# Input stage of a hybrid attention block: x tiles 6 and 7 load into a free buffer, ahead of the turned blocks

## The chip, the cores and the metric

The kernel runs on one NeuronCore of a Trainium2 chip. The metric is the time of the whole launch in microseconds (us) on the device, the median of several runs. Five engines run their own instruction streams in order: TensorE (PE in the profile, PEld for its weight loads), VectorE (DVE), ScalarE (ACT), GpSimd (POOL) and SyncE (SP), which here issues nearly all DMAs. They meet by semaphores.

## The reference

One layer over x of 2048 rows by 1024 columns:

```python
h = rms_norm(x, norm_gain[layer])
proj = h @ w_in[layer]
qa, ka, va, qb, kb, vb, ga, gb, mg = jnp.split(proj, split_idx, axis=-1)
...
ya = ya.reshape(bsz, S, A_WIDTH) * jax.nn.silu(ga)
...
merged = gates[:, :, 0] * br_a + gates[:, :, 1] * br_b
x = x + merged @ w_out[layer]
```

Between the split and the gates lie two attention mixers with normed q and k. What matters here comes before them: each row of x is scaled by one over its root mean square, each column by a gain, and the result h, transposed, is the operand of every projection; and the first of these projections is that of the gate path `silu(ga)`.

## The kernel before, in words

The program has an input stage, then 14 units of attention (projection, norm, scores, output), then the merge and output projection. All tensors that TensorE multiplies are split in two fp16 parts, high and low, and each product is three matmuls (high by high, high by low, low by high). The input stage makes the transposed, normed h in two tensors, XH (high) and XL (low), in four quarters of 512 rows of x, and runs 16 gate products with them: quarter q by gate weight c is gate 4q + c, 24 matmuls each (8 of XH by the weight's high part gh, 8 of XH by its low part gl, 8 of XL by gh). SP loads x twice: as 16 tiles `xt` of 128 rows (x 0 to 15, 512 KB each), and already transposed as "turned blocks" `xq` (t1, t2, t3: one for each of the quarters 1 to 3, four loads of 512 KB each). Names of the steps, with their lines in the profile:

- **sq.t**: ScalarE squares x tile t and sums along its rows (L492; tile 3 on VectorE, L488). **st, ln, nw**: mean, and one over the root, for a quarter's four tiles (L496, L264 and L265, L278 to L280; in quarters 2 and 3 all on VectorE, L509 to L513).
- **dg.t**: that scale on the diagonal of a 128 by 128 tile (L523 on ScalarE, L521 for the first quarter).
- Quarter 0 has no turned block: TensorE turns x tiles 0 to 3 by a matmul with dg (**tr**, L535), and **h0**, **l0** split the result (L538, L541).
- **rb.t**: in the other quarters TensorE spreads the scales of tile t over all partitions, ones by dg (L529, `s<-dg,ones`; a record pair each). **mu**: VectorE multiplies a chunk of the turned block by gain and scales (L545, eight a quarter), **hi.q.j** on ScalarE (L549) and **lo.q.j** on VectorE (L553) make XH and XL from it, four each a quarter.
- **mm** are the gates' matmuls (L372), **th** the tanh of a gate's sum on ScalarE (L382), **gt** its product on VectorE (L389), and then SP stores it (L395). The store's tile `yo` has three buffers, so a later th waits for a store to have landed.
- **w0 to w3** are the gate weights' loads (L323), squared (**gq**), split into gh (L358) and gl (L362). **u**, four loads of 384 KB (L187), is the weights of the first attention unit: **uq** squares them (L222), **um** sums the squares over partitions on TensorE (L198, `pt<-wsq,ones`), **up** makes a scale, **uh** and **ul** split them (L239, L245).

x tiles rotate through six buffers (`XR_BUFS`), turned blocks through two (`XT_BUFS`): t1 and t2 have their own, t3 takes t1's, when all lo.1 are done. So x 6 to 9 need the buffers of tiles 0 to 3, which are free once TensorE has turned them eight times (the last four turns are those of column chunk 7), and later tiles those whose square is done. The order of the loads is given by the list `X_LD`; the order on ScalarE and VectorE is written out in `X_SEQ`; TensorE's and SP's steps are placed by `Order`, a list scheduler in the kernel's own program that works with assumed durations (`X_US`) and emits each step at its planned time. A load is there an issue step on "S" and a transfer on "Q". In the program before, an issue step waited only for its buffer in the plan, not for the issue before it in the list, so a load whose buffer was planned to come free late was emitted behind others that follow it in `X_LD`.

The engines then run these streams in order, waiting where data are not there. On SP, a DMA also waits for the DMA eight places before it to land.

Of the kernel before, what the change touches and what calls it, by code (L numbers as in the profile page):

```python
# [88 lines left out]
WO_AT = 2.0, 5.5  # L89
M_AT = {0: (1.0, (5.0, 6.6, 8.2, 9.8, 11.4, 13.0, 14.6)), 1: (1.0, (6.5, 8.7, 10.9, 13.1, 15.3, 17.5, 19.7)),  # L90
        7: (.7, (3.5, 5.4, 7.3, 9.2, 11.1, 13.5, 26.4))}
X_LD = ("g", 0, 1, "w0", 2, 3, "w1", "w2", "w3", 4, 5, 6, 7, "t1", 8, 9, 10, 11, "t2", 12, 13, 14, 15, "u", "t3")
X_US = dict(look=0.25, land=4.95, next=1.24, late=.12, sq=1.25, dq=1.45, st=.17, ln=.42, nw=.6, ng=2.1, dg=.27, rb=.26, tr=.26, h0=.72, l0=.72,
            mu=.8, hi=1.08, lo=1.38, pw=1.25, gq=1.25, gh=1.15, gl=1.3, mm=.217, th=.69, gt=.69, us=1.03, uh=.94, ul=1.05)
X_SQV = (3,)
X_SEQ = {
# [21 lines left out]
def block_kernel(tc, x, xt, w_units, w_gate, w_mrg, w_out, w_bra, w_brk, gain, qkg, sink, bias_a, bias_b, b_merge, out):  # L118
    nc = tc.nc
    V = nc.vector  # L120
    A = nc.scalar
    G = nc.gpsimd
    T = nc.tensor
# [168 lines left out]
    gp = gps.enter_context(tc.tile_pool(name="gp", bufs=1, side="right"))  # L292
# [136 lines left out]
    st = ExitStack()  # L429
    sp0 = st.enter_context(tc.tile_pool(name="sp0", bufs=1))  # L430
# [7 lines left out]
    xts, xtt, xq, rr_, rs_ = {}, {}, {}, {}, {}  # L438
# [2 lines left out]
    gsum = []  # L441

    def x_load(t):
        xts[t] = sp0.tile([128, D], F32, name="xt", bufs=XR_BUFS)
        nc.sync.dma_start(out=xts[t][:], in_=x[128 * t:128 * t + 128, :])

    def t_load(q, i):
        if i == 0:
            xtt[q] = sp0.tile([128, NCH, 512], F32, name="xq", bufs=XT_BUFS)
        nc.sync.dma_start(out=xtt[q][:, i:i + 2, :], in_=xt[i:i + 2, :, 512 * q:512 * q + 512].rearrange("c p t -> p c t"))  # L450

# [29 lines left out]
    def x_square(t, dve):  # L481
        q, i = divmod(t, 4)
        if q not in rs_:
            rs_[q] = sp0.tile([128, 4], F32, name="xss", bufs=4)
        o = rs_[q][:, i:i + 1]
        if dve:
            jk = sp0.tile([128, D], F16, name="jv")
            V.tensor_tensor_reduce(out=jk[:], in0=xts[t][:], in1=xts[t][:], scale=1.0, scalar=0.0,  # L488
                                   op0=OP.mult, op1=OP.add, accum_out=o)
        else:  # L490
            jk = sp0.tile([128, D], F16, name="jk")
            A.activation(jk[:], xts[t][:], AF.Square, accum_out=o)  # L492
# [84 lines left out]
    class Order:  # L577
# [37 lines left out]
    od = Order()  # L615
    od.free["Q"] = X_US["land"] - X_US["next"]
    us_ = X_US
    n = 0
    for k in X_LD:
        if k == "g":  # L620
            at(.001 * n, gain_load)
            od.end["ld", "g", 0] = 4.0, "Q"
            n += 1
            continue
        kind = k[0] if isinstance(k, str) else "x"
        for i in {"t": (0, 2, 4, 6), "u": (0, 1, 2, 3)}.get(kind, (0,)):
            free = []
            if kind == "u":
                f, args = w_load, (0, (i,))
            elif kind == "w":  # L630
                f, args = g_load, (int(k[1]),)
            elif kind == "t":
                q = int(k[1])
                f, args = t_load, (q, i)
                if i:
                    free = [("is", k, i - 2)]
                elif q > XT_BUFS:
                    free = [("lo", q - XT_BUFS, j) for j in range(4)]
            else:
                f, args = x_load, (k,)  # L640
                if k >= XR_BUFS:
                    free = [("tr", k - XR_BUFS, c) for c in range(NCH)] if k < XR_BUFS + 4 else [("sq", k - XR_BUFS)]
            od.add(("is", k, i), "S", .45, free, n, f, *args)
            od.add(("ld", k, i), "Q", us_["next"] * (.75 if k == "u" else 1), [("is", k, i)], n, lambda: None)
            n += 1
        if k == "t1":
            od.add(("sl",), "S", 1.0, [], n, small_loads)
            n += 1
    od.add(("g0",), "A", .4, [("ld", "g", 0)], -99, gain_square)
    od.add(("g1",), "T", .15, [("g0",)], -99, gain_sum)  # L650
# [1 line left out]
    for q in range(4):  # L652
# [667 lines left out]
    for u in range(NU + 1):  # L1320
        t = 8 * u
# [553 lines left out]
    yf, gt, mf = {}, {}, {}  # L1875
# [174 lines left out]
    class Branch(Seven):  # L2050
        n, mm_us = 7, MM1
# [65 lines left out]
    class Out(Seven):  # L2117
        n, mm_us = 7, MM
# [77 lines left out]
    for s in range(8):  # L2196
        p = pos[0]
# [92 lines left out]
```

## Time and profile before

| what | us |
|---|---|
| median of 3 runs (lowest, highest) | 1907.14 (1906.85, 1911.3) |
| the profiled execution: its time | 1908.05 |
| its span, first to last instruction | 1906.0 |
| busy in the span: TensorE, VectorE, ScalarE, GpSimd | 1870.3, 1489.0, 1241.2, 579.4 |
| first matmul of the first attention unit starts | 118.14 |
| TensorE busy ahead of it | 98.58 |

The profile gives one execution, in us from the first instruction. In a row of a timeline the first number is the start, the second the length, and `xN` the number of instructions merged into the row; in brackets stands the idle time before it and what ended it. A matmul of a float32 operand leaves two records, so four rb are `x8`. In the rows of waits stand the waiting engine and line, what ended the wait, the total, the number of waits and the longest. `granted clock` (PEclk) is TensorE's clock as a share of full speed.

### The profile page before, as it was taken

To read this page: it belongs to the slowest core of one execution; us is meant where nothing else is said; L and a number is where in the kernel's file an instruction comes from. 1 tells how busy PE (TensorE), PEld (TensorE's weight loads), DVE (VectorE), ACT (ScalarE), POOL (GpSimd) and SP (SyncE) were. 2 spreads that over 40 slices of the span, in tenths; PEclk is the share of its full clock that TensorE was granted. 3 is DMA by queue.
4 is the path that set the end of the run, shared out by engine and by line. 5 is a ranking of instruction groups with operands and counts; after the bars stand their busy time and mean duration, and the time that the engine had idled before them with its cause. 6 is when DMAs were issued, how large, how long until landed. Compare 5 with 4: busy or idle time off the path is not lost.

```text
span 1906.0 us, 51076 instructions
## 1 busy us (share of the span) xinstructions
PE 1870.3 (98%) x19238; PEld 1437.1 (75%) x19238; DVE 1489.0 (78%) x3824; ACT 1241.2 (65%) x2994; POOL 579.4 (30%) x1363
## 2 busy tenths in 40 slices
PE   6999999999999999999999999999999999999999
PEld 4457897788999989998999989844444446776775
DVE  4738987998788788888788888866788754987885
ACT  6628776887767677677777676656567865433341
POOL 0013343344355344544345444520000000322121
PEclk8999999999999999999999999999999999999999
DMA  9326988897697786966878857667768758954552
GB/s 345 105 87 128 210 157 183 146 207 162 143 197 155 152 173 150 175 160 148 178 146 174 174 120 154 151 212 276 205 210 244 234 176 270 303 159 121 143 152 73
DMA packets 644263, 336.18 MB, mean 176 GB/s; under 512 B 459312, under 2 KB 590256, under 8 KB 641584
## 3 DMA queue, kind: packets, MB, share of 16 engines
q1 hardware_dynamic: 643872, 332.66, 71.6%
q8 instruction: 150, 2.46, 0.6%
q14 instruction: 97, 0.79, 0.1%
q10 hardware_dynamic: 144, 0.26, 0.0%
HBM read 146.95 MB, written 75.76 MB: 117 GB/s over the span
## 4 chain that ended last, share of the span: by engine, by line
PE 91%; DMA 5%; DVE 2%; ACT 1%; issue 1%; POOL 0%; SPq 0%; DVEq 0%; ACTq 0%; POOLq 0%
PE pj L802 42%; PE fps L1736 16%; PE fps L2063 8%; PE fps L2148 7%; PE s L955 5%; PE pv L1004 4%; PE pj L372 3%; DMA kq<-spl 2%; PE pj L313 2%; DMA pt<-p 2%; PE fps L313 1%; DMA xt<-in_x_dram 1%; PE pt L1068 1%; PE pv L372 1%; DMA bigl<-sd 1%
## 5 line engine op out<-in xcount | busy, mean ns | idle before, releaser
L802 PE MATMUL pj<-wl,XH 128*128 128x128 f16 (+2 forms) x2816 | 715.2, 268 | 0.0
L802 PE MATMUL pj<-wh,XL 128*128 128x128 f16 (+2 forms) x2816 | 711.6, 269 | 0.0
L802 PE MATMUL pj<-wh,XH 128*128 128x128 f16 (+2 forms) x2816 | 708.6, 268 | 0.0
L802 PEld LDWEIGHTS <-XH 128*128 128x128 f16 x5632 | 574.8, 112 | 54.1
L802 PEld LDWEIGHTS <-XL 128*128 128x128 f16 x2816 | 315.6, 112 | 23.8
L970 DVE CUSTOM_DVE_ANT_0 pr<-s,b,ubuf 128x256 f32<-128x256 f32 (+3 forms) x512 | 218.9, 465 | 41.9 <-PE s L955 39.0
L987 DVE SCALAR_TENSOR_TENSOR p<-pr,p 128x512 f16<-128x512 f32 (+2 forms) x256 | 194.9, 762 | 47.7 <-ACT p L983 44.5
L869 POOL TENSOR_TENSOR rw<-rw,g 128x128 f32<-128x128 f32 (+1 forms) x224 | 148.9, 684 | 197.0 <-DVE rw L862 171.8
L2073 POOL TENSOR_TENSOR g<-g,t 128x512 f32<-128x512 f32 x32 | 48.3, 1510 | 487.1 <-DMA g<-mgd 347.2
L1736 PEld LDWEIGHTS <-wh 128*128 128x128 f16 x952 | 93.2, 98 | 112.1 <-issue 2.0
L820 ACT ACTIVATE rw<-pj 128x256 f32<-128x256 f32 (+1 forms) x224 | 87.3, 390 | 132.5 <-PE pj L802 131.6
L884 POOL COPY spl<-spl 128x256 f16<-128x256 f16 (+1 forms) x224 | 97.0, 462 | 245.5 <-DVE spl L879 244.7
L983 ACT ACTIVATE p<-pr 128x512 f16<-128x512 f32 (+2 forms) x256 | 157.6, 616 | 9.5 <-DMA pt<-p 5.0
L955 PE MATMUL s<-kq 128*128 128x128 f16 (+1 forms) x1984 | 151.2, 217 | 4.2 <-DMA kq<-spl 3.1
L2063 PE MATMUL fps<-y,bigh 128*128 128x128 f16 x1792 | 153.4, 219 | 0.0
L2063 PE MATMUL fps<-y,bigl 128*128 128x128 f16 x896 | 151.7, 219 | 0.0
L2148 PE MATMUL fps<-WO,mf 128*128 128x512 f16 x660 | 147.5, 379 | 0.0
L955 PEld LDWEIGHTS <-kq 128*128 128x128 f16 x2016 | 131.0, 98 | 20.4 <-issue 5.4
L2063 PEld LDWEIGHTS <-bigh 128*128 128x128 f16 x1792 | 139.0, 98 | 7.3
L1004 PE MATMUL pv<-vt,pt 128*128 128x65 f16 (+1 forms) x2784 | 131.6, 193 | 6.2 <-DMA pt<-p 6.2
L1004 PEld LDWEIGHTS <-pt 128*128 128x128 f16 x3024 | 119.8, 97 | 20.8 <-DMA pt<-p 7.7
L875 ACT ACTIVATE spl<-rw 128x512 f16<-128x512 f32 (+1 forms) x112 | 72.0, 643 | 79.8 <-POOL vt L831 70.4
(288 smaller groups left out, 3767.5 us busy)
## 6 DMA issues: line engine op xcount, KB each, us to landing
wraw<-in_w_units_dram SPq DMA_DIRECT2D x56, 384.0 KB, 4.7
g<-mgd SPq DMA_DIRECT2D x64, 256.0 KB, 5.7
mgd<-t SPq DMA_DIRECT2D x43, 256.0 KB, 3.6
wraw<-in_w_mrg_dram SPq DMA_DIRECT2D x41, 256.0 KB, 4.8
zd<-z SPq DMA_DIRECT2D x128, 66.0 KB, 2.0
zz<-zd SPq DMA_DIRECT2D x64, 132.0 KB, 3.3
xt<-in_x_dram SPq DMA_DIRECT2D x16, 512.0 KB, 6.8
ytd<-yo SPq DMA_DIRECT2D x32, 256.0 KB, 3.3
```

Source lines behind the costliest of these rows:

```text
L802: out.append(lambda lhs=lhs, rhs=rhs, ch=ch, a=a, b=b, k=k: T.matmul(ps[:, a:b], lhsT=lhs[:, ch, :], rhs=rhs[:, ch, a:b], start=(k == 0), ...
L820: A.activation(self.rw[:, n * i:n * i + n], self.ps[i][:, :n], AF.Copy)
L869: G.tensor_tensor(q[:, i, :un.nq, :], q[:, i, :un.nq, :], g, OP.mult)
L884: G.tensor_copy(sp[:, i, nh:, :, :], sp[:, i, nq:nh, ::-1, :])
L955: T.matmul(self.sv[j][:, o:o + k1 - k0], lhsT=q[:, h, :], rhs=kt[:, un.nq + kh + v * un.nk, k0:k1], start=(v == 0), stop=(v == 1))
L970: V.tensor_tensor_reduce(out=self.pv[:, j, self.p0:self.p0 + W], in0=self.sv[j], in1=un.bias[:, self.h0 + j, self.b0:self.b0 + W], scale=I ...
L983: A.activation(self.sp[:, :128 * n], self.pr, AF.Copy, scale=PSC)
L987: V.scalar_tensor_tensor(self.sp[:, 128 * n:], self.pr, PSC, self.sp[:, :128 * n], OP.mult, OP.subtract)
L1004: T.matmul(self.po[:, j, :w], lhsT=p[:, n * j + s, :], rhs=un.v[key][:, vh, c0:c0 + w], start=(k == 0 and s == 0), stop=(k == 2 and s == n ...
L1736: T.matmul(b[k][:], lhsT=w[:, i, ch, :], rhs=xform(PROD[i][0], lo, ch, q), start=(i < 3 and n == 0), stop=(n == 11), skip_group_check=True)
L2063: out.append(lambda p=p, c=c, wl=wl, yl=yl, n=n: T.matmul(ps[:, 128 * p:128 * p + 128], lhsT=w[wl][:, i, c, p, :], rhs=y[:, yl, c, :], sta ...
L2148: out.append(lambda p=p, ml=ml, wl=wl, k=k: T.matmul(ps[:], lhsT=m[:, ml, p, :], rhs=WO[:, i, wl, p, :], start=(fresh and k == 0), stop=(k ...
```

## The change

x tiles 6 and 7 no longer wait for the buffers of tiles 0 and 1. They load into the second turned-block buffer, that of t2, which is empty then, ahead of t1; t2's loads then wait for sq.6 and sq.7. The other tiles rotate as before without 6 and 7, so x 8 to 11 take the places of tiles 0 to 3. In the planner each load now also follows the one ahead of it in the list, on SP and in the transfer, so SP issues them in the order of `X_LD`; the three small loads stand behind u, and an issue step needs 2.4 us of notice. um additionally waits, in the plan, for gate 8's ninth matmul. In `X_SEQ` sq.15, uh.1 and a few of mu and lo change places.

```diff
+X_SPARE = (6, 7)
 X_LD = ("g", 0, 1, "w0", 2, 3, "w1", "w2", "w3", 4, 5, 6, 7, "t1", 8, 9, 10, 11, "t2", 12, 13, 14, 15, "u", "t3")
-X_US = dict(look=0.25, land=4.95, next=1.24, late=.12, sq=1.25, dq=1.45, st=.17, ln=.42, nw=.6, ng=2.1, dg=.27, rb=.26, tr=.26, h0=.72, l0=.72,
+X_US = dict(look=0.25, land=4.95, next=1.3, iss=2.4, late=.12, sq=1.25, dq=1.45, st=.17, ln=.42, nw=.6, ng=2.1, dg=.27, rb=.26, tr=.26, h0=.72, l0=.72,
...
     def x_load(t):
-        xts[t] = sp0.tile([128, D], F32, name="xt", bufs=XR_BUFS)
-        nc.sync.dma_start(out=xts[t][:], in_=x[128 * t:128 * t + 128, :])
+        if t in X_SPARE:
+            for q in (1, 2):
+                if q not in xtt:
+                    xtt[q] = sp0.tile([128, NCH, 512], F32, name="xq", bufs=XT_BUFS)
+            k = 2 * X_SPARE.index(t)
+            xts[t] = xtt[2][:, k:k + 2, :].rearrange("p c t -> p (c t)")
+        else:
+            xts[t] = sp0.tile([128, D], F32, name="xt", bufs=XR_BUFS)[:]
+        nc.sync.dma_start(out=xts[t], in_=x[128 * t:128 * t + 128, :])
...
-                if k >= XR_BUFS:
-                    free = [("tr", k - XR_BUFS, c) for c in range(NCH)] if k < XR_BUFS + 4 else [("sq", k - XR_BUFS)]
-            od.add(("is", k, i), "S", .45, free, n, f, *args)
-            od.add(("ld", k, i), "Q", us_["next"] * (.75 if k == "u" else 1), [("is", k, i)], n, lambda: None)
+                j = rot.index(k) - XR_BUFS if k in rot else -1
+                if j >= 0:
+                    free = [("tr", rot[j], c) for c in range(NCH)] if rot[j] < 4 else [("sq", rot[j])]
+            if kind == "t" and k == "t2":
+                free = free + [("sq", t) for t in X_SPARE]
+            od.add(("is", k, i), "S", .45, free + prev[:1], n, f, *args)
+            od.add(("ld", k, i), "Q", us_["next"] * (.75 if k == "u" else 1), [("is", k, i)] + prev[1:], n, lambda: None)
+            prev = [("is", k, i), ("ld", k, i)]
             n += 1
-        if k == "t1":
-            od.add(("sl",), "S", 1.0, [], n, small_loads)
+        if k == "u":
+            od.add(("sl",), "S", 1.5, prev[:1], n, small_loads)
+            prev[0] = ("sl",)
             n += 1
...
-    od.add(("um",), "T", .15, [("uq", i) for i in range(4)] + [("gp", 1)], 0, w_sum, 0)
+    od.add(("um",), "T", .15, [("uq", i) for i in range(4)] + [("gp", 1), ("mm", 8, 8)], 0, w_sum, 0)
```

What the engines' streams become, at the places that the prediction speaks of. First SP, from x 4 and 5 to the first gate's store; `xt<-in_x_dram` is an x tile, `xq<-in_xt_dram` a turned block's loads, `wraw` is u, `qg`, `snk`, `bmt` are the small loads, and `xN` counts rows alike. Before:

```order
L445 DMA xt<-in_x_dram 128x1024 x2
L450 DMA xq<-in_xt_dram 128x2x512 x4
L453 DMA qg<-in_qkg_dram 128x256
L454 DMA snk<-in_sink_dram 128x8
L455 DMA bmt<-in_b_merge_dram 128x16
L450 DMA xq<-in_xt_dram 128x2x512 x4
L187 DMA wraw<-in_w_units_dram 128x768 x4
L445 DMA xt<-in_x_dram 128x1024 x10
L395 DMA gtd_87<-yo 128x512
```

and now:

```order
L453 DMA xt<-in_x_dram 128x1024 x2
L453 DMA xq<-in_x_dram 128x1024 x2
L458 DMA xq<-in_xt_dram 128x2x512 x4
L453 DMA xt<-in_x_dram 128x1024 x4
L458 DMA xq<-in_xt_dram 128x2x512 x4
L453 DMA xt<-in_x_dram 128x1024 x4
L188 DMA wraw<-in_w_units_dram 128x768 x4
L461 DMA qg<-in_qkg_dram 128x256
L462 DMA snk<-in_sink_dram 128x8
L463 DMA bmt<-in_b_merge_dram 128x16
L396 DMA gtd_87<-yo 128x512
```

x 6 and 7 (now `xq<-in_x_dram`) move from behind u to ahead of t1, x 8 to 15 from behind u to both sides of t2, and u and the small loads to the end.

Second ScalarE, from hi.1 to th.4, th.3 and th.2 (`dg<-idf` is dg of tiles 8 to 11, `jk,xss<-xt` the squares of tiles 12 to 15, `wl,wsq<-wraw` uq). Before:

```order
L549 ACTIVATE XH<-xq 128x2x512 x4
L523 ACTIVATE dg<-idf,xss 128x128
L382 ACTIVATE yo<-pj,gih_235 128x512
L523 ACTIVATE dg<-idf,xss 128x128 x3
L222 ACTIVATE wl,wsq<-wraw 128x768
L492 ACTIVATE jk,xss<-xt 128x1024 x4
L382 ACTIVATE yo<-pj,gih_235 128x512
L382 ACTIVATE yo<-pv,gih_287 128x512 x2
```

and now (one buffer number in a name differs, and so do the line numbers):

```order
L557 ACTIVATE XH<-xq 128x2x512 x4
L531 ACTIVATE dg<-idf,xss 128x128
L383 ACTIVATE yo<-pj,gih_277 128x512
L531 ACTIVATE dg<-idf,xss 128x128 x2
L500 ACTIVATE jk,xss<-xt 128x1024
L531 ACTIVATE dg<-idf,xss 128x128
L223 ACTIVATE wl,wsq<-wraw 128x768
L500 ACTIVATE jk,xss<-xt 128x1024 x3
L383 ACTIVATE yo<-pj,gih_225 128x512
L383 ACTIVATE yo<-pv,gih_277 128x512 x2
```

One square, sq.15, moves ahead of the last dg (dg.8) and of uq.3.

Third TensorE at um. Before, it stood in the XL part of gate 6:

```order
L372 LDWEIGHTS gh
L372 MATMUL pj<-XL,gh 128x512
L198 MATMUL pt<-wsq,ones 128x4
L372 LDWEIGHTS gh
L372 MATMUL pj<-XL,gh 128x512
```

and now behind the first XH by gl matmul of gate 8:

```order
L373 MATMUL pj<-XH,gh 128x512
L373 LDWEIGHTS gl
L373 MATMUL pj<-XH,gl 128x512
L199 MATMUL pt<-wsq,ones 128x4
L373 LDWEIGHTS gl
```

um moves 36 gate matmuls back. Besides, rb.8 to 11 stand six gate matmuls later, behind gate 4's last gl product, and rb.12 to 15 two later, behind gate 7's last XH by gh product. TensorE's other rows, up to the program's end, stand as they stood.

More of the change, by code (lines that the diff above doesn't have):

```diff
@@ L443, in x_load @@
     def x_load(t):
-        xts[t] = sp0.tile([128, D], F32, name="xt", bufs=XR_BUFS)
-        nc.sync.dma_start(out=xts[t][:], in_=x[128 * t:128 * t + 128, :])
+        if t in X_SPARE:
[7 more added lines that the diff above has]
+        nc.sync.dma_start(out=xts[t], in_=x[128 * t:128 * t + 128, :])
     def t_load(q, i):
-        if i == 0:
+        if q not in xtt:
             xtt[q] = sp0.tile([128, NCH, 512], F32, name="xq", bufs=XT_BUFS)
@@ L487, in x_square @@
             jk = sp0.tile([128, D], F16, name="jv")
-            V.tensor_tensor_reduce(out=jk[:], in0=xts[t][:], in1=xts[t][:], scale=1.0, scalar=0.0,
+            V.tensor_tensor_reduce(out=jk[:], in0=xts[t], in1=xts[t], scale=1.0, scalar=0.0,
                                    op0=OP.mult, op1=OP.add, accum_out=o)
@@ L491, in x_square @@
             jk = sp0.tile([128, D], F16, name="jk")
-            A.activation(jk[:], xts[t][:], AF.Square, accum_out=o)
+            A.activation(jk[:], xts[t], AF.Square, accum_out=o)
     def x_stats(q, a, b):
@@ L590, in start @@
                 return None
-            return max([self.free.get(eng, 0.0)] + [self.end[d][0] + (0 if self.end[d][1] == eng else X_US["late"]) for d in deps])
+            return max([self.free.get(eng, 0.0)] + [self.end[d][0] + (0 if self.end[d][1] == eng else X_US["iss" if eng == "Q" else "late"]) for d in deps])
         def run(self):
@@ L618, in block_kernel @@
     n = 0
+    prev = []
+    rot = [t for t in range(16) if t not in X_SPARE]
     for k in X_LD:
```

8 rows, old and new, of the table X_SEQ are left out of this document.

## The prediction

> **What bounds the kernel now.** I read the busy time by stretches first, then TensorE's waits, then the chain of waits, then the timelines of the input stage.
>
> The stretches (length, then busy time and instructions of PE, PEld, DVE, ACT and POOL, granted clock, DMA share, GB/s):
>
> ```profile
> 0.00:118.14 118.14, 98.58 (x480) 51.61 (x481) 65.89 (x138) 65.64 (x113) 1.96 (x10) 0.96 0.51 191
> 118.14:300.00 181.86, 175.18 (x2268) 148.40 (x2267) 151.60 (x413) 132.72 (x318) 68.79 (x164) 1.00 0.81 161
> ```
>
> TensorE sets the time; of its idle time, 19.6 us lie in the input stage. Its waits there that bear on the change:
>
> ```profile
> PE s L529 <- ACT dg L523: 8.7, 1, 8.7
> PE pt L198 <- ACT wl L222: 1.7, 1, 1.7
> ```
>
> The first is rb.4 to 7 waiting for dg.4, the second um waiting for the last square of the first unit's weights. The chain says what stands behind them (start, length, what):
>
> ```profile
> 26.44 9.09 DMA xt<-in_x_dram
> ...
> 40.01 2.08 PE s L529 x8
> ...
> 60.64 5.58 DMA gtd<-yo
> ...
> 72.98 45.33 PE pj L372 x210
> ```
>
> So rb.4 waits for x tile 7, issued at 26.44 and landed at 35.53. The second root is the store of gate 4, issued at 60.64 and landed at 66.22. From 72.98 TensorE runs through: 210 products in 45.33, 0.216 us each. Why x 6 and 7 come late stands in SP's timeline:
>
> ```profile
> 5.25 1.55 SPq L445 DMA_DIRECT2D xt<-in_x_dram  x2
> 7.76 4.20 SPq L450 DMA_DIRECT2D xq<-in_xt_dram  x4
> ...
> 25.12 18.29 SPq L445 DMA_DIRECT2D xt<-in_x_dram  x10
> ...
> 56.45 3.33 SPq L450 DMA_DIRECT2D xq<-in_xt_dram  x4
> ```
>
> x 4 and 5 are issued from 5.25, then t1, the small loads, t2 and u; x 6 leads the ten of 25.12.
>
> **The change part by part.** *x 6 and 7 ahead of t1.* They take the places in the queue of t1's first two loads. The first of those, issued at 7.76, needed
>
> ```profile
> xq<-in_xt_dram SPq DMA_DIRECT2D x1, 512.0 KB, 10.3
> ```
>
> so x 6 lands near 7.76 + 10.3 = 18.1. The rate, from the stretches:
>
> ```profile
> 20.00:30.00 10.00, 10.00 (x51) 4.86 (x51) 5.81 (x8) 4.10 (x7) 0.00 (x0) 1.00 1.01 372
> 30.00:40.00 10.00, 1.33 (x7) 0.39 (x4) 0.96 (x5) 5.24 (x11) 0.00 (x0) 0.67 1.03 408
> ```
>
> A load of 512 KB (0.524 MB) takes 1.28 us at 408 GB/s and 1.41 at 372; I take 1.31 (400). x 7 lands near 19.4, t1 by 24.6, x 8 to 11 by 29.9, t2 by 35.1, x 12 to 15 by 40.4, and u, 0.98 each, by 44.3. At 372 GB/s u ends 17 x 0.10 + 4 x 0.08 = 2.0 later, at 46.3.
>
> ScalarE's timeline gives the durations (idle time before in brackets):
>
> ```profile
> 22.91 1.10 ACT L492 ACTIVATE jk<-xt 128x1024 f16<-128x1024 f32 x1
> ...
> 34.33 1.06 ACT L492 ACTIVATE jk<-xt 128x1024 f16<-128x1024 f32 x1 [10.23 <-DMA xt<-in_x_dram]
> ...
> 35.62 1.06 ACT L492 ACTIVATE jk<-xt 128x1024 f16<-128x1024 f32 x1
> ...
> 36.80 1.06 ACT L492 ACTIVATE jk<-xt 128x1024 f16<-128x1024 f32 x1
> ...
> 39.57 1.26 ACT L523 ACTIVATE dg<-idf,xss 128x128 f32<-128x128 f32 x4
> ...
> 45.62 1.28 ACT L382 ACT_TABLE_LOAD   x1
> ...
> 47.50 3.88 ACT L549 ACTIVATE XH<-xq 128x1024 f16<-128x1024 f32 x4
> ...
> 53.02 0.83 ACT L222 ACTIVATE wl<-wraw 128x768 f16<-128x768 f32 x1
> ```
>
> A square takes 36.80 - 35.62 = 1.18. sq.5 starts at 22.91; with x 6 and 7 landed, sq.6, 7 and 4 follow at once, and sq.4 starts at 22.91 + 3 x 1.18 = 26.4. From sq.4's start to dg.4 it is 39.57 - 36.80 = 2.8, so dg.4 starts at 29.2, and dg.7 ends at 30.5. TensorE:
>
> ```profile
> 19.62 1.13 PE L535 MATMUL s<-dg,xt 128*128 128x128 f32 x8 [0.51 <-DVE XL L541]
> ...
> 30.09 1.24 PE L372 MATMUL pv<-XH,gh 128*128 128x512 f16 x5
> 40.01 2.08 PE L529 MATMUL s<-dg,ones 128*128 128x128 f32 x8 [8.68 <-ACT dg L523]
> 41.88 1.49 PE L372 MATMUL pv<-XH,gh 128*128 128x512 f16 x3
> ...
> 45.16 1.89 PE L372 MATMUL pv<-XL,gh 128*128 128x512 f16 x8
> ...
> 54.22 1.05 PE L529 MATMUL s<-dg,ones 128*128 128x128 f32 x8
> 55.12 1.46 PE L372 MATMUL pj<-XH,gl 128*128 128x512 f16 x6
> ```
>
> It comes to rb.4 at 30.09 + 1.24 = 31.3, after dg.7. **The wait of 8.7 goes whole**; x 7 could land as late as 26 before it came back.
>
> With it goes a slow stretch. The granted clock:
>
> ```profile
> 32.00:34.00 2.00, 0.00 (x0) 0.00 (x0) 0.00 (x0) 0.00 (x0) 0.00 (x0) 0.87 1.02 407
> 34.00:36.00 2.00, 0.00 (x0) 0.00 (x0) 0.00 (x0) 1.53 (x3) 0.00 (x0) 0.50 1.03 412
> ...
> 42.00:43.00 1.00, 1.00 (x4) 0.33 (x3) 0.88 (x2) 1.00 (x2) 0.00 (x0) 0.50 0.44 78
> ...
> 44.00:45.00 1.00, 1.00 (x7) 0.45 (x5) 1.00 (x3) 0.97 (x3) 0.00 (x0) 1.00 0.90 340
> ```
>
> It fell to 0.50 some 2.2 into the wait (0.87 is the mean of 1.5 us at full rate and 0.5 at half), and was 1.00 again by 44. rb.4 to 7 took 41.88 - 40.01 = 1.87, where rb.8 to 11 took 55.12 - 54.22 = 0.90: 0.97 lost. The 11 products behind took 45.16 - 41.88 = 3.28 where 11 x 0.216 = 2.38: 0.90 lost. **1.9 in all.** [...]
>
> *Does the second quarter keep up?* TensorE does rb.4 to 7 (0.90), the 19 products left of gate 2 and the 24 of gate 3, and reaches gate 4 at 31.3 + 0.9 + 43 x 0.216 = 41.5. t1 lands 2.6 later than now, at 24.6, hidden: VectorE multiplies only after rb.7, at 32.2, and six of its eight products take 4.0, so they are there when hi.1 wants them:
>
> ```profile
> 42.12 4.04 DVE L545 SCALAR_TENSOR_TENSOR xq<-xq,gs,s 128x512 f32<-128x512 f32 x6 [1.14 <-PE s L529]
> ```
>
> ScalarE's table load was 45.62 - 39.57 = 6.05 after dg.4, so it comes at 35.3, and the four hi.1 end 47.50 + 3.88 - 45.62 = 5.8 later, at 41.1; the last is needed at 41.5 + 6 x 0.216 = 42.8. rb.8 to 11 now stand behind gate 4's eight gl products, 41.5 + 16 x 0.216 = 45.0; dg.8 has sq.15 ahead of it (x 15 landed 40.4) and ends near 43.9. Both covers are 1 to 2 us thick; cost nothing. At 372 GB/s sq.15 still has its tile at 42.1.
>
> *u later, behind x 15.* uq.3 came 53.02 - 47.50 = 5.5 after the first hi.1. Now that is 37.2 + 5.5 + 1.18 for sq.15 = 43.9, and u lands at 44.3: ScalarE waits 0.4. Behind uq.3 stand sq.13, 14 and 12 and th.4, which starts at 44.3 + 0.83 + 3 x 1.18 = 48.7. TensorE is through gate 4 at 41.5 + 28 x 0.216 + 0.9 = 48.5, so th.4 falls when its product does, 10.5 earlier than now:
>
> ```profile
> 59.20 0.69 ACT L382 ACTIVATE yo<-pj,gih 128x512 f32<-128x512 f32 x1 [0.67 <-PE pj L372]
> ...
> 66.32 0.69 ACT L382 ACTIVATE yo<-pj,gih 128x512 f32<-128x512 f32 x1 [3.63 <-DMA gtd<-yo]
> ...
> 71.38 0.39 ACT L523 ACTIVATE dg<-idf,xss 128x128 f32<-128x128 f32 x1
> ```
>
> *um later.* Its wait of 1.7 goes: it now stands in gate 8, long after uq.1. But both waits had one root: th.5 waits for gate 4's store, which lies behind t3 (56.45) in the DMA queue. Store and t3 move with th.4 and lo.1, 10.5 earlier, so dg.12, which ended at 71.38 + 0.39 = 71.8, ends at 61.3. TensorE reaches rb.12, now behind gate 7's eight XH products, at 41.5 + 80 x 0.216 + 0.9 = 59.7. **A wait of about 1.7 at rb.12 takes the place of um's.** Its bounds: 0 (the store no longer meets t3, 60.64 + 5.58 being mostly queue) and 1.7 + 2.0 = 3.7 (372 GB/s). I take 1.7, the value that follows from the rows unchanged.
>
> Behind it:
>
> ```profile
> 93.77 2.87 DVE L245 SCALAR_TENSOR_TENSOR wl<-wraw,ubuf,wh 128x768 f16<-128x768 f32 x3
> 96.55 1.22 DVE L553 TENSOR_TENSOR XL<-xq,XH 128x1024 f16<-128x1024 f32 x1
> ```
>
> ul ended at 96.6, unit 0 began at 118.14: um can be 20 us later for nothing. The last lo.3 (97.8) was 20.4 before the stage's end, and keeps that distance if VectorE moves with TensorE, as its order, nearly the same, lets it. In the rest of the program every engine keeps its order, so what is saved ahead of unit 0 is saved at the end.
>
> **Sum:** 8.7 + 1.9 + 1.7 - 1.7 = 10.6. The profiled execution, 1908.05 (span 1906.0 and 2.05 around it), becomes 1897.4; it lies 0.9 over the median of 1907.14, which becomes **1896.5**.
>
> **The rivals.** *Late loads* (faster, by less): u.3 lands 2 to 5 us later. Each us is a us of th.4, of the store, of dg.12 and of TensorE at rb.12. For it: the 372 GB/s of 20 to 30, and SP's new waits (x 8 for tile 0's last turn, in the row of 19.62, t2 for sq.6 near 25); against it: when SP comes to the first of these waits, t1 keeps the engines busy until 24.6, and to the second, x 8 to 11 until 29.9. Time 1898.5 to 1901.4, say 1899.5. [...]
>
> *The gap comes back* (within 0.3%): the wait at rb.12 grows until the clock falls, as it did 2.2 into the 8.7 but not in um's 1.7, and 1.9 is paid again. With u 3.5 late that is 3.5 + 1.9: 1901.9. It needs loads of 1.49, 353 GB/s. Or the change does not do what it says, and rb.4 waits as now because x 6 and 7 land after 35: 1907. Against it: they are the ninth and tenth large x loads in SP's order.
>
> *Slower:* u.3, last of 21 loads behind x 6, holds ScalarE's in-order queue so long that th.4 is later than 59.2. The point is u.3 at 44.3 + 10.6 - 1.9 = 53.0; at 59 the time is 1913. That takes 2.05 us a load, 256 GB/s. For it: the queue ran thin (78 GB/s from 42 to 43) when x 14 and 15 waited for squares, and ten of the 21 now wait for a turn or a square. Against it: from 20 to 40 the DMA share was 1.01 and 1.03 with x 6 to 10 under such waits.
>
> **How the numbers follow.** Forecast 0.68 (own range 1894.5 to 1898.5: no wait at rb.12, or 3.7), late loads 0.17, the gap back or not gone 0.11, slower 0.04. Under 0.3%, 5.7 us, this kernel's measurement tells nothing from no change. Faster: 0.68 + 0.17 = 0.85; within 0.3%: 0.11; slower: 0.04. The range, 1894 to 1901.5, takes in the first two.
>
> **What would show it.** Right: no wait of rb.4 on dg; clock 1.00 from 30 to 50; th.4 near 48.7; a wait of 0 to 3.7 of rb.12 on dg in place of um's; unit 0 from 107.5. Wrong: sq.6 after 27, u.3 after 47, a wait of gate 4 on hi.1 or of gate 12 on lo.3, or unit 0 at 107.5 and an end that does not move with it.

## The result, and the profile after

The changed kernel takes **1896.93 us** in the median (1894.78 to 1902.09, 7 runs), beside 1907.14 (1906.75 to 1911.71, 7 runs) for the kernel before: a ratio of 0.9946, with a 95% interval of 0.993 to 0.9961. Predicted were 1896.5 and a range of 1894 to 1901.5, so the forecast came about. The profiled execution took 1895.46, its span is 1893.2 (1906.0 before), and the first matmul of unit 0 starts at 107.13 instead of 118.14.

The two stretches, then four of the short ones of the prediction (columns as there: length, busy time of PE, PEld, DVE, ACT and POOL, granted clock, DMA share, GB/s):

```profile
0.00:107.13 107.13, 96.30 (x480) 50.45 (x481) 65.90 (x138) 65.41 (x113) 1.96 (x10) 1.00 0.56 210
107.13:300.00 192.87, 188.09 (x2394) 157.24 (x2393) 160.54 (x436) 140.00 (x338) 72.82 (x178) 1.00 0.83 167
...
32.00:34.00 2.00, 2.00 (x11) 0.88 (x9) 2.00 (x4) 1.97 (x4) 0.00 (x0) 1.00 1.05 389
34.00:36.00 2.00, 2.00 (x11) 0.87 (x9) 2.00 (x5) 1.95 (x5) 0.00 (x0) 1.00 1.05 410
...
20.00:30.00 10.00, 10.00 (x50) 4.69 (x49) 7.05 (x12) 9.63 (x19) 0.00 (x0) 1.00 1.04 397
30.00:40.00 10.00, 10.00 (x52) 5.08 (x51) 8.06 (x22) 9.40 (x14) 0.00 (x0) 1.00 1.04 399
```

TensorE had 19.6 us without work in the stage, and now has 10.8. Where it was idle and its clock at 0.50, between 32 and 36, it is busy throughout at 1.00. ScalarE, busy for 4.10 and 5.24 of the two stretches of ten before, is now busy for 9.63 and 9.40: it has x tiles to square. The DMA moves what it moved (397 and 399 GB/s beside 372 and 408); only what comes first has changed.

From 23.5 us to unit 0, one wait of TensorE on another engine is left:

```profile
PE s L537 <- ACT dg L531: 1.8, 1, 1.8
```

It is rb.12 waiting for dg.12, the one that the prediction put in um's place. TensorE's and ScalarE's timelines at the places of the prediction's steps:

```profile
30.79 1.05 PE L537 MATMUL s<-dg,ones 128*128 128x128 f32 x8
31.68 0.81 PE L373 MATMUL pv<-XH,gh 128*128 128x512 f16 x3
...
44.42 1.05 PE L537 MATMUL s<-dg,ones 128*128 128x128 f32 x8
...
61.11 1.16 PE L537 MATMUL s<-dg,ones 128*128 128x128 f32 x8 [1.82 <-ACT dg L531]
...
107.13 0.33 PE L817 MATMUL pj<-wh,XH 128*128 128x384 f16 x1
```

```profile
22.57 1.09 ACT L500 ACTIVATE jk<-xt 128x1024 f16<-128x1024 f32 x1
...
45.20 0.84 ACT L223 ACTIVATE wl<-wraw 128x768 f16<-128x768 f32 x1 [1.28 <-DMA wraw<-in_w_units_dram]
...
49.44 0.67 ACT L383 ACTIVATE yo<-pj,gih 128x512 f32<-128x512 f32 x1
...
55.91 0.69 ACT L383 ACTIVATE yo<-pj,gih 128x512 f32<-128x512 f32 x1 [3.01 <-DMA gtd<-yo]
```

rb.4 to 7 (30.79) stand right behind the first five products of gate 2 and take 31.68 - 30.79 = 0.89, not 1.87. The lower rows are sq.5, uq.3, th.4 and th.5. uq.3 still waits for u, and th.5 for the store of gate 4.

One thing has to be set apart. Profiles do not begin the stage at the same moment: sq.5, the last step that has the same work ahead of it in all kernels, starts anywhere between 22.57 and 24.19 in the fourteen profiles of this study. Times are therefore counted from sq.5's start from here on. Unit 0 then starts at 118.14 - 22.91 = 95.23 before and at 107.13 - 22.57 = **84.56** after: the stage became 10.67 shorter. The two spans differ by 12.8; the rest is the 0.34 of that start and 1.8 behind unit 0, where both programs are the same and one execution differs from the next (a second profile of the changed kernel, below, has 1.1 more there than the kernel before).

### The profile page after: what moved, and what is told of

It is laid out like the page before. It is cut to its first block, busy times and chain, and to the rows that moved or that the text cites. A ratio compares the mean times of both kernels' runs of the same rounds, so it can differ in the third digit from the quotient of the medians.

```text
span 1893.2 us, 51081 instructions
## 1 busy us (share of the span) xinstructions
PE 1867.7 (99%) x19238; PEld 1436.2 (76%) x19238; DVE 1489.5 (79%) x3824; ACT 1239.9 (65%) x2994; POOL 579.6 (31%) x1363
## 4 chain that ended last, share of the span: by engine, by line
PE 88%; DMA 6%; DVE 2%; ACT 2%; issue 2%; POOL 1%; SPq 0%; DVEq 0%; POOLq 0%; ACTq 0%
PE pj L817 42%; PE fps L1751 16%; PE fps L2078 8%; PE fps L2163 8%; PE s L970 5%; PE pv L1019 4%; DMA kq<-spl 2%; PE pj L373 2%; PE pj L314 2%; PE fps L314 1%; DMA pt<-p 1%; PE pt L1083 1%; DVE pr L985 1%; DMA bigl<-sd 1%; DMA wraw<-in_w_units_dram 0%
```

## The experiments

The theory at first was the prediction's: the wait on x 6 and 7, with its slow clock, makes the 10.6, and what is left at rb.12 hangs on u (u, uq.3, th.4, store, th.5). After the first four runs a second theory was set against its last part: the store of gate 4 stands behind t3's four loads in the queue, so th.5 follows the issue of t3, which waits for lo.1, and so for rb.7 and mu.1, whatever th.4 does.

**The load order without the spare buffer.**

```diff
-X_SPARE = (6, 7)
+X_SPARE = ()
```

> The change without the spare buffer: x 6 and 7 load into the rotating buffers of tiles 0 and 1 again; the planner's order, um and all else as changed. My theory: SP stands at x 6 from 7.6 until tile 0 has been turned for the last time (19.6), and the DMA queue runs empty near 16.5. x 7 lands near 25, still in time for rb.4 (no wait, or under 0.5), t1 by 30.5, x 8 to 11 by 36, u by 50.5. sq.11 waits 5 and hi.1 behind it, so TensorE waits 1 to 2 at gate 4, and rb.12 waits 5 to 6 behind the later u; unit 0 begins at 112 to 113.5, and the time is near 1902: half of the gain. Rival, the order alone carries the change: unit 0 at 107, time 1896.5 to 1897. Rival, the buffer alone carries it: unit 0 near 118, 1907.

Measured: 1904.09 us, ratio 0.9974 (0.9962 to 0.9985); unit 0 at 90.24, 4.99 earlier than before. The size is near what was expected, the place is not. SP's four loads of x 4 to 7 took 16.3 us to issue, since x 6 had to wait for tile 0's buffer, the later tiles came late, and TensorE waited at gate 4 instead. Its row there, VectorE's rows, and the granted clock around that wait:

```profile
46.26 3.85 PE L373 MATMUL pj<-XH,gh 128*128 128x512 f16 x8 [4.27 <-DVE xh L519]
```

```profile
32.75 4.04 DVE L553 SCALAR_TENSOR_TENSOR xq<-xq,gs,s 128x512 f32<-128x512 f32 x6 [1.57 <-PE s L537]
43.29 0.17 DVE L504 TENSOR_SCALAR xss<-xss 128x4 f32<-128x4 f32 x1 [6.51 <-ACT jk L500]
43.37 1.40 DVE L553 SCALAR_TENSOR_TENSOR xq<-xq,gs,s 128x512 f32<-128x512 f32 x2
```

```profile
45.00:45.50 0.50, 0.00 (x0) 0.00 (x0) 0.21 (x1) 0.50 (x2) 0.00 (x0) 0.53 1.06 426
...
51.50:52.00 0.50, 0.50 (x3) 0.20 (x2) 0.50 (x2) 0.32 (x2) 0.00 (x0) 0.64 1.09 394
```

In VectorE's stream the mean of quarter 2 (L504, held for 6.51 by the squares of x 8 to 11, of which sq.11 waited 7.54 for its tile) stood ahead of the last two mu.1 that gate 4 needs, and they started behind it, at 43.37. A late tile of the *next* quarter held the present one. With the 4.27 the clock fell to 0.50, from 45.0 to 51.9.

**The spare buffer without the planner's new rules** (no `prev`, old assumed times, um and the small loads in their old places, `X_SEQ` as before).

```diff
-            od.add(("is", k, i), "S", .45, free + prev[:1], n, f, *args)
+            od.add(("is", k, i), "S", .45, free, n, f, *args)
...
-    od.add(("um",), "T", .15, [("uq", i) for i in range(4)] + [("gp", 1), ("mm", 8, 8)], 0, w_sum, 0)
+    od.add(("um",), "T", .15, [("uq", i) for i in range(4)] + [("gp", 1)], 0, w_sum, 0)
```

> The spare buffer alone: x 6 and 7 load into t2's buffer ahead of t1, but the planner keeps its old rules, ScalarE and VectorE their old order, um its old place, and u and the small loads stay ahead of x 8 to 15. My theory: no wait of rb.4 (8.7 and 1.9 gone). x 11 lands near 34 instead of 30.6, sq.11 waits 4, hi.1 comes near 41 to 45, so TensorE waits 1 at gate 4 and 1 to 3 at rb.8; u is early. um waits for uq.1 again, 1.5 to 2.5. Unit 0 begins at 110 to 111.5, time 1899.5 to 1901. Rival, getting x 6 and 7 early is all there is in the change: unit 0 at 107 to 107.8, 1897. Rival, the old order of the other loads costs what the buffer wins: 115 or later, 1904.

Measured: 1904.52 us, ratio 0.9977 (0.9967 to 0.9988); unit 0 at 91.10, 4.13 earlier than before: later than expected. TensorE's row of um and ScalarE's of th.5:

```profile
64.97 0.38 PE L199 MATMUL pt<-wsq,ones 128*128 128x4 f32 x2 [3.57 <-ACT wl L223]
```

```profile
61.59 0.69 ACT L383 ACTIVATE yo<-pj,gih 128x512 f32<-128x512 f32 x1 [5.35 <-DMA gtd<-yo]
```

um waited for 3.57, twice as long as before, because th.5 ahead of uq.1 waited for 5.35; four waits of some 0.4 at gate 4, one of 0.72 at rb.8, and another slow stretch of the clock make up the rest. So neither half has the whole gain, and 4.99 + 4.13 = 9.12 is less than 10.67: each half removes the 8.7 at rb.4 and then loses part of it to a wait further on that the other half removes.

**The slow clock alone.** The kernel before, with forty gate matmuls more ahead of rb.4, in the gap; their result is never read.

```diff
             rps[q] = s_p.tile([128, 512], F32, name="s")
+            if q == 1:
+                fill = norm_bank[0]()
+                for k in range(40):
+                    T.matmul(fill[:], lhsT=gw[0][0][:, k % NCH, :], rhs=XH[:, k % NCH, 0:512], start=True, stop=True)
```

> The kernel before, with 38 matmuls of 128x512 (8.2 us) into a PSUM bank that nothing reads, on TensorE ahead of rb.4, so that the wait of 8.7 is filled with work. My theory: the clock stays at 1.00 from 30 to 50; rb.4 to 7 take 0.9 instead of 1.87, the 11 products behind 2.4 instead of 3.28. But the 1.9 does not all reach the end: th.4 then waits for sq.12 (58.4), so the store and uq.1 come only 0.8 earlier and um waits 2.8 instead of 1.7. Unit 0 at 117.3, time 1906.3. Rival, the slow clock costs its whole 1.9: unit 0 at 116.3, 1905.3. Rival, the lower clock of the rows costs nothing: rb.4 to 7 take 1.87 as before, unit 0 at 118.1.

The kernel that ran has forty of them, which took 8.80, not the 38 of the expectation.

Measured: 1908.32 us, ratio 0.999 (0.9979 to 1.0001); unit 0 at 95.22, where it was (95.23). The clock stayed at 1.00, and the 11 products behind rb.7 ran at their normal pace. TensorE's timeline shows where that went:

```profile
40.90 1.36 PE L533 MATMUL s<-dg,ones 128*128 128x128 f32 x8 [0.21 <-ACT dg L523]
...
54.26 1.16 PE L533 MATMUL s<-dg,ones 128*128 128x128 f32 x8 [0.56 <-ACT dg L523]
...
70.42 0.39 PE L198 MATMUL pt<-wsq,ones 128*128 128x4 f32 x2 [2.26 <-ACT wl L222]
```

rb.8 now waits 0.56, and um 2.26 instead of 1.69, because th.5 came when it came before (43.40 after sq.5; 43.41 before). A faster TensorE met the same store sooner.

**th.5 in a buffer of its own**, so that it does not wait for a store.

```diff
-            th.append(gp.tile([128, 512], F32, name="yo", bufs=3))
+            th.append(sp0.tile([128, 512], F32, name="y5") if m is None and (q, c) == (1, 1) else gp.tile([128, 512], F32, name="yo", bufs=3))
```

> The change, with a buffer of its own for th.5's tile, so that th.5 does not wait for gate 4's store, which lies behind t3. My theory: the store is the root of the wait of rb.12. th.5 starts at 52.9 instead of 55.9, dg.12 ends near 58.6, ahead of TensorE at 59.1, and the wait of 1.8 goes: unit 0 at 105.3 instead of 107.1, time 1.8 under the change's, near 1895. Rival, another wait takes its place (th.6 for a buffer, hi.2 for mu, gate 8 for lo.2): unit 0 at 106.5 to 107.1.

Measured: **1895.16 us** (1894.25 to 1896.97, 6 runs), ratio 0.9926 (0.9914 to 0.9938); unit 0 at 82.49, 2.07 earlier than in the changed kernel. ScalarE's row of th.5 (it writes `y` now), and TensorE's of rb.12:

```profile
53.16 0.69 ACT L383 ACTIVATE y<-pj,gih 128x512 f32<-128x512 f32 x1
```

```profile
59.87 1.05 PE L537 MATMUL s<-dg,ones 128*128 128x128 f32 x8
```

Neither waits. TensorE has no wait on another engine from sq.5 to unit 0. That the wait at rb.12 hangs on th.5's buffer, and so on a store, is shown.

**um back in its old place.**

```diff
-    od.add(("um",), "T", .15, [("uq", i) for i in range(4)] + [("gp", 1), ("mm", 8, 8)], 0, w_sum, 0)
+    od.add(("um",), "T", .15, [("uq", i) for i in range(4)] + [("gp", 1)], 0, w_sum, 0)
```

> The change with um back in its old place, in gate 6. Counted from the start of sq.5, because the start of the stage moves by up to 1.4 from run to run: unit 0 begins 84.6 after it in the changed kernel, 95.2 before. My theory: um and rb.12 wait for the same chain (th.5, dg, uq.1, dg.12). um then waits 2.5 for uq.1, rb.12 not at all, and unit 0 begins at 85.2 to 85.4: moving um is worth 0.7. Rival, um's wait and rb.12's are two separate costs: 86.3. Rival, moving um is worth nothing: 84.6.

Measured: 1901.77 us (three runs, 1897.17 to 1903.92), ratio 0.9948 (0.9912 to 0.9983); unit 0 at 84.58, where the changed kernel has it. TensorE:

```profile
59.71 0.38 PE L199 MATMUL pt<-wsq,ones 128*128 128x4 f32 x2 [1.82 <-ACT wl L223]
```

The same 1.82 now stands at um, and rb.12 no longer waits. Moving um is worth nothing in the stage: whichever comes first takes the wait.

**t1 ahead of x 6 and 7.**

```diff
-4, 5, 6, 7, "t1", 8,
+4, 5, "t1", 6, 7, 8,
```

> The change with t1's four loads ahead of x 6 and 7, which still go into t2's buffer. My theory: x 7 only has to land before ScalarE comes to sq.7 (25.0); behind t1 it lands at 24.7. No wait of rb.4, unit 0 at 84.4 to 84.9 after sq.5's start, as in the change. Rival, being ahead of the turned block matters: x 7 lands 5 later and rb.4 waits 1 or more, unit 0 at 85.6 or later.

Measured: 1897.33 us, ratio 0.9926 (0.9896 to 0.9956); unit 0 at 84.17, a wait of 1.41 at rb.12 and none at rb.4. The four places ahead of t1 are not needed; the buffer and the place ahead of x 8 are enough.

**uq.3 behind th.2**, which takes u off th.4's way.

```diff
-dg.8 uq.3 sq.13 sq.14 sq.12 th.4 th.3 th.2 uq.2
+dg.8 sq.13 sq.14 sq.12 th.4 th.3 th.2 uq.3 uq.2
```

> The change with uq.3 moved on ScalarE from ahead of sq.13 to behind th.2, so that sq.13, 14, 12 and th.4 no longer wait for u (1.3 in the changed kernel). First theory, that of the prediction: each us of th.4 is a us of the store, of dg.12 and of TensorE at rb.12. th.4 comes 1.3 earlier, rb.12 waits 0.5 instead of 1.8, unit 0 at 83.3 after sq.5's start. Second theory, after the run with the filled gap: the store lands when t3, issued ahead of it, has passed, whatever th.4 does. th.5 starts at 33.1 to 33.4 after sq.5's start as now, rb.12 waits 1.5 to 1.8, unit 0 at 84.2 to 84.6.

Measured: 1897.17 us, ratio 0.9922 (0.9894 to 0.9951); unit 0 at 85.21, 0.65 later than in the changed kernel. ScalarE's rows of th.4 and th.5:

```profile
48.32 0.69 ACT L383 ACTIVATE yo<-pj,gih 128x512 f32<-128x512 f32 x1 [0.74 <-PE pj L373]
...
56.54 0.69 ACT L383 ACTIVATE yo<-pj,gih 128x512 f32<-128x512 f32 x1 [3.91 <-DMA gtd<-yo]
```

th.4 came 1.32 earlier after sq.5 and the store was issued 1.30 earlier, but th.5 0.43 later (against a second profile of the changed kernel, below: 0.58 and 0.57 earlier, 0.32 later). An earlier th.4 buys nothing: the first theory's 83.3 falls.

**u later, first attempt:** two loads of 512 KB ahead of u, into columns of XL that are overwritten later.

```diff
+                        for j in range(2):
+                            junk(j)
+                        w_load(u, parts)
```

> The change with two more loads of 512 KB ahead of u (into parts of XL that are written later, so they change no result); u lands 2.6 later. First theory, that of the prediction: th.4, the store, dg.12 and TensorE at rb.12 all come 2.6 later, rb.12 waits 4.4, the clock begins to fall; unit 0 at 87.2 to 88.5 after sq.5's start. Second theory: the store still lands with t3 (issued 23.6 after sq.5's start); gate 6 waits 1 for gt.4, rb.12 about 1 less; unit 0 at 84.6 to 85.1.

Measured: 1901.19 us, ratio 0.995 (0.9915 to 0.9986); unit 0 at 87.65. This number lies where the first theory put it, for another reason, so the run decides nothing. TensorE:

```profile
42.88 1.02 PE L373 MATMUL pv<-XL,gh 128*128 128x512 f16 x4 [2.83 <-DMA XL<-in_x_dram]
44.35 1.44 PE L373 MATMUL pv<-XL,gh 128*128 128x512 f16 x3 [0.45 <-DMA XL<-in_x_dram]
```

These are matmuls of gate 3, which read other columns of XL than the loads write, and yet they wait for the loads: TensorE itself was held for 3.28. The likely reason, not shown, is that the program's own dependence tracking took the column ranges for overlapping ones.

**u later, second attempt:** eight loads of 128 KB, each into one row of columns, which adds no wait on the other engines.

```diff
+    def u_load(u, parts):
+        if parts == (0,):
+            for j in range(8):
+                nc.sync.dma_start(out=(XL, XH)[j % 2][:, j | 1, 1536:2048].bitcast(F32), in_=x[128 * j:128 * j + 128, 0:256])
+        w_load(u, parts)
```

> The changed kernel with eight loads of 128 KB more on SyncE's queue just ahead of u (into columns of the halves of the fourth block, which nothing reads before they are written again; no other engine's waits change): at some 400 GB/s u comes 2.6 us later, so uq.3 about 25.2 after sq.5 in place of 22.6 and th.4 about 29.3 in place of 26.9. First theory (the prediction's: u holds uq.3, that th.4, that the store, that th.5 and rb.12): the wait of rb.12 grows to 4.0-4.4, unit 0 starts 86.7-87.2 after sq.5 (84.56 in the changed kernel's profile), time about 1899. Second theory (the store of gate 4 lands behind t3's loads whenever it is issued, and t3 goes out when lo.1 ends): th.5 stays within 0.7 of 33.3 after sq.5, unit 0 84.4-85.3, time about 1897.

Measured: 1900.87 us, ratio 0.9956 (0.9938 to 0.9974); unit 0 at 85.87. uq.3 started at 25.53 after sq.5 and th.4 at 29.78, both 2.9 later than in the changed kernel's first profile; th.5 only 1.3 later:

```profile
49.11 0.84 ACT L223 ACTIVATE wl<-wraw 128x768 f16<-128x768 f32 x1 [4.77 <-DMA wraw<-in_w_units_dram]
...
58.23 0.69 ACT L383 ACTIVATE yo<-pj,gih 128x512 f32<-128x512 f32 x1 [1.41 <-DMA gtd<-yo]
```

It lies between the two theories' intervals. u has slack, but not the whole 2.9.

**Nine matmuls (1.94 us) ahead of rb.4, and the same nine ahead of rb.8.** Both are the changed kernel with

```diff
             rps[q] = s_p.tile([128, 512], F32, name="s")
+            if q == 1:
+                fill = norm_bank[0]()
+                for k in range(9):
+                    T.matmul(fill[:], lhsT=gw[0][0][:, k % NCH, :], rhs=XH[:, k % NCH, 0:512], start=True, stop=True)
```

where the second has `q == 2`.

> The changed kernel with nine matmuls of 512 columns more on TensorE (0.216 each from the second on: 1.94 us; their result is never read) just ahead of rb.4-7; no load and no other engine's order is touched. Second theory (what counts is when rb.7 ends and mu.1 begins): mu.1, t3's issue, th.5 and rb.12 all come 1.94 later, the wait of rb.12 stays at 1.6-2.0, unit 0 starts 86.2-86.7 after sq.5, time +1.9 against the changed kernel. First theory (u's landing sets th.5): th.5 stays, the wait of rb.12 falls to nearly nothing, unit 0 84.6-85.1.

> The same nine matmuls (1.94 us, never read) just ahead of rb.8-11, that is behind mu.1's start and ahead of the wait of rb.12. Second theory: the wait of rb.12 takes them in: it falls from 1.82 to under 0.3, th.5 stays within 0.5 of 33.3 after sq.5, unit 0 starts 84.5-85.0 after sq.5, time within 0.5 of the changed kernel's. Rival (TensorE is itself the bound of the stage, and its waits follow its own lateness): the wait stays, unit 0 86.2-86.7, time +1.9.

Measured: 1898.67 us, ratio 0.9941 (0.9926 to 0.9955), unit 0 at 85.75 for the first; 1896.83 us, ratio 0.993 (0.9914 to 0.9947), unit 0 at 85.94 for the second. rb.12 in the one and in the other:

```profile
62.77 1.16 PE L541 MATMUL s<-dg,ones 128*128 128x128 f32 x8 [1.04 <-ACT dg L531]
```

```profile
62.70 1.16 PE L541 MATMUL s<-dg,ones 128*128 128x128 f32 x8 [1.23 <-ACT dg L531]
```

Both miss every interval that was named for unit 0 and for the wait. mu.1 starts 1.95 later in the first and in its place in the second, as meant, but in both 0.6 to 0.8 of the 1.94 disappears in the wait, and 1.1 to 1.4 reach unit 0. The second theory fails in its sharp form: what TensorE loses behind mu.1 counts about as much as what it loses ahead of it.

**The changed kernel once more.**

> The changed kernel itself once more, beside the three others, to learn how far one profile repeats. Both theories: unit 0 starts 84.3-84.8 after sq.5 (84.56 in its first profile), the wait of rb.12 is 1.6-2.0, time 1895-1898. Against both: unit 0 off by more than 0.5, which would take the meaning from the differences of half a microsecond between the other kernels.

Measured: 1899.33 us (1894.4 to 1901.23), ratio 0.994 (0.9922 to 0.9958); unit 0 at 84.67, the wait at rb.12 1.85. The two profiles of this kernel agree to 0.11 in the stage, though not in each step: th.4 starts at 26.87 in the first and at 26.13 in the second. The medians of the launches do not resolve this: in this group 1896.83 to 1900.87 stand beside stages of 84.67 to 85.94 in another order.

**What the runs say together.** In 13 of the 14 profiles the start of unit 0 is 82.5 to 83.4 of TensorE's work plus what it lost on the way. Slow clock counts as half the work time at 0.50 (in the kernel before rb.4 to 7 took 1.87 at 0.50, rb.8 to 11 0.90 at 1.00).

| kernel | unit 0 after sq.5 | TensorE's waits | slow clock | added matmuls | rest |
|---|---|---|---|---|---|
| before | 95.23 | 8.68 + 1.69 | 1.87 | | 83.0 |
| changed | 84.56 | 1.82 | | | 82.7 |
| changed, again | 84.67 | 1.85 | | | 82.8 |
| order alone | 90.24 | 4.27 + 0.15 | 2.8 | | 83.0 |
| slow clock filled | 95.22 | 0.21 + 0.56 + 2.26 | | 8.8 | 83.4 |
| th.5 own buffer | 82.49 | none | | | 82.5 |
| um back | 84.58 | 1.82 | | | 82.8 |
| t1 first | 84.17 | 1.41 | | | 82.8 |
| uq.3 later | 85.21 | 2.06 + 0.22 | | | 82.9 |
| loads into XL | 87.65 | 2.83 + 0.45 | 1.6 | | 82.8 |
| u later | 85.87 | 1.56 + 1.40 | | | 82.9 |
| matmuls ahead of rb.4 | 85.75 | 1.04 | | 1.94 | 82.8 |
| matmuls ahead of rb.8 | 85.94 | 1.23 | | 1.94 | 82.8 |

The spare buffer alone leaves 83.6 by the same count (91.10, waits of 5.75, 1.7 slow), so 0.8 of it is not found.

The rest of the wait at rb.12 follows th.5: rb.12 starts 5.19 to 5.20 after th.5 wherever it waits for dg.12 (eight profiles). And th.5 starts when gate 4's store has landed. When is that? Here are, after sq.5, the starts of t3's issue and of the store's, the time at which t3's last load has landed (its issue and what it took from there), and the start of th.5, in the profiles where th.5 waits for the store:

| kernel | t3 issued | store issued | t3 landed | th.5 | th.5 behind t3's issue |
|---|---|---|---|---|---|
| before | 33.54 | 37.73 | 42.6 | 43.41 | 9.9 |
| slow clock filled | 33.90 | 37.30 | 42.6 | 43.40 | 9.5 |
| order alone | 30.69 | 35.29 | 39.7 | 40.54 | 9.9 |
| spare buffer alone | 27.67 | 30.84 | 36.9 | 37.66 | 10.0 |
| uq.3 later | 23.67 | 26.98 | 33.0 | 33.77 | 10.1 |
| t1 first | 23.03 | 27.21 | 32.2 | 32.95 | 9.9 |
| changed, again | 23.05 | 27.55 | 32.7 | 33.45 | 10.4 |
| um back | 23.03 | 27.58 | 32.3 | 33.02 | 10.0 |
| changed | 23.62 | 28.28 | 32.6 | 33.34 | 9.7 |
| matmuls ahead of rb.4 | 24.43 | 28.93 | 33.8 | 34.52 | 10.1 |
| matmuls ahead of rb.8 | 23.62 | 28.93 | 33.9 | 34.72 | 11.1 |
| u later | 23.62 | 31.19 | 33.8 | 34.65 | 11.0 |

For the changed kernel the two times to landing are these, of t3's last load (issued at 49.36) and of the store (at 50.85):

```profile
xq<-in_xt_dram SPq DMA_DIRECT2D x1, 512.0 KB, 5.8
```

```profile
gtd<-yo SPq DMA_DIRECT2D x1, 256.0 KB, 5.0
```

In all twelve rows th.5 starts 0.7 to 0.8 after t3's last load has landed, and the store itself landed 0.6 to 0.8 after it, though it was issued 2.6 to 6.1 ahead of that landing. So the store lands behind t3, and issuing it earlier gains nothing. That much of the second theory stands, in the last two rows too: there it was t3 that landed later.

What fails is that t3 follows mu.1 one for one. With the matmuls ahead of rb.4 mu.1 came 1.95 later, but t3's issue only 0.8 to 1.4, by which profile of the changed kernel is taken. The reason stands in VectorE's row of gt.1, which comes ahead of the last three lo.1; here in the changed kernel and with the matmuls:

```profile
42.04 0.69 DVE L390 SCALAR_TENSOR_TENSOR yo<-yo,pj 128x512 f32<-128x512 f32 x1 [0.97 <-ACT yo L383]
```

```profile
43.33 0.69 DVE L390 SCALAR_TENSOR_TENSOR yo<-yo,pj 128x512 f32<-128x512 f32 x1
```

VectorE had waited there for th.1, for 0.97 and 0.53 in the two profiles, and that slack took up its part of the 1.95.

With u later, t3 was issued when it was before, at 23.62, but its first load landed 6.3 after its issue in place of 5.0, and the others followed at the same distance of 1.3: it stood in the queue behind u's later loads and the stores of gates 0 and 1, which landed at 28.0 and 28.9. So, as these landings read, u comes through to th.5 by way of t3, with 1.3 of its 2.9. With the matmuls ahead of rb.8, t3 was issued at 23.62 too, and its loads took 7.4 us to land (median of four) and 5.8 in the changed kernel. Why they took longer there stays open.

## Why the prediction was right, step by step

- *The wait of 8.7 goes whole, and 1.9 of slow clock with it.* Right. rb.4 to 7 come at 30.79 (predicted 31.3) and take 0.89, and the clock is 1.00 where it was 0.50. As a sum over TensorE's losses this is what happened: 8.68 + 1.87 + 1.69 - 1.82 = 10.42, beside 10.67 measured. As a list of separate gains it is not: the 1.9 alone, without an earlier x 7, is worth 0.0, since it comes back as waits at rb.8 and um. It counted here because t3 and the store moved forward with it.
- *The second quarter keeps up.* Right: gate 4 reached at 40.96 (41.5), rb.8 to 11 at 44.42 (45.0), both without a wait. The run with the order alone shows how near the edge that was: with sq.11 at 38.57, the in-order VectorE held gate 4 for 4.27. The prediction gave this no price.
- *u lands at 44.3, ScalarE waits 0.4, th.4 at 48.7.* u landed 0.9 later and the wait was 1.28, th.4 at 49.44. In the sum this cost nothing, and here a step was wrong: "Each us is a us of th.4, of the store, of dg.12 and of TensorE at rb.12". By it, the 0.7 by which th.4 came late would have made the wait at rb.12 2.4; it was 1.82. With u 2.9 later, 1.3 came through; with uq.3 out of the way and th.4 1.3 earlier, nothing was gained. What counts is when t3's last load lands: the store lands 0.6 to 0.8 behind it, and u has slack until its own loads hold up t3's.
- *A wait of about 1.7 at rb.12 takes the place of um's.* Right, 1.82; the size came out because t3 moved with lo.1, by 10.3 (10.5 forecast). "Both waits had one root" is shown twice: with um put back the 1.82 stands at um, and with th.5 in its own buffer there is no wait. The edit of um is by itself worth nothing.
- *"What is saved ahead of unit 0 is saved at the end."* Right within what can be told: 10.67 in the stage and 0.9946 of the time, which is 10.3 at 1907.14, with 7.4 to 13.3 for the interval.
- The rivals: late loads, the gap coming back and the slow case did not occur. The rate was 397 and 399 GB/s from 20 to 30 and from 30 to 40, near the 400 that the forecast took.

The version with th.5 in its own buffer is the best that was run. Its stage, profiled once, is 2.1 to 2.2 shorter than in the two profiles of the changed kernel; its time, 1895.16 with a ratio of 0.9926 (0.9914 to 0.9938), is below the changed kernel's 1896.93 in the median, but its interval overlaps with the changed kernel's (0.993 to 0.9961), so that the launches alone do not show this gain.

## What to carry to other kernels

Cost an edit by the engine that sets the end: its start of the next stage is its work plus its waits, and a term counts only if no wait behind it grows by the same amount. For each wait removed, ask what its release depended on; if two waits have one root, moving either consumer is worth nothing, and giving the producer a free buffer is worth both. A store that stands behind bulk loads in one queue landed here 0.6 to 0.8 us after the last of them, so a buffer that waits for it inherits the time at which they land.

## What the runs showed of the hardware that was not expected

**The slow stretches of the clock.** Read in half microseconds, with the mean of a slice that mixes 1.00 and 0.50 giving the moment in it, the clock was at 0.50 from 33.46 to 43.70 before (10.24), from 45.03 to 51.86 with the order alone (6.83), from 66.12 to 69.53 with the spare buffer alone (3.41), and from 44.11 to 47.53 with the loads into XL (3.42): three, two, one and one times 3.41, to within 0.01. The fall had no fixed place in these four. In the kernel before and with the order alone it came within the wait, 2.1 and 3.0 after its start. With the loads into XL it came 1.2 us after the wait of 2.83 had ended (and inside the 0.45 that followed), and with the spare buffer alone 1.1 us after um had ended the wait of 3.57, at 64.97:

```profile
65.50:66.00 0.50, 0.50 (x4) 0.22 (x3) 0.50 (x1) 0.36 (x1) 0.00 (x0) 1.00 0.00 0
66.00:66.50 0.50, 0.50 (x4) 0.16 (x2) 0.10 (x1) 0.44 (x1) 0.00 (x0) 0.62 0.00 0
...
69.50:70.00 0.50, 0.50 (x5) 0.37 (x5) 0.09 (x1) 0.00 (x0) 0.00 (x0) 0.97 0.00 0
```

Nor did full speed come back with the work: it came 3.7 after the end of the wait in the kernel before, 5.6 with the order alone, 4.6 with the spare buffer alone, and 3.2 after the end of the 0.45 with the loads into XL. From sq.5 on, waits of up to 2.26 cost no clock in the other profiles; those of 2.83 to 4.27 cost 1.6 to 2.8, and the 8.68 cost 1.9. What sets the moments of the fall and of the return is not shown: these are four cases, and no run was made for it.

**A store behind loads.** The store of gate 4, 256 KB, took 4.96 to 6.7 us from issue to landing where it left within 5.3 us of t3's four loads of 512 KB, and 3.4 where it left 7.6 behind them; each time it landed 0.6 to 0.8 after the last of them. The stores of gates 0 and 1, with no load beside them, took 2.4 in the kernel before.
